# Two transformer blocks on one core: seven shared 4 KB weight slots, deferred decays and transposes, and softmaxes used one step later

## The chip, the cores and the metric

The kernel runs on one core of a Trainium2 chip. The metric is device time in microseconds (us). TensorE (PE) multiplies, VectorE (DVE), ScalarE (ACT) and GpSimd (POOL) do the element-wise work, and SyncE (SP) issues nearly all DMAs, in the order of its queue. On each engine the instructions run in one fixed order.

## The reference, cut to what matters

The input is one sequence of 256 tokens with 1024 features. A first block of two hybrid layers and a second block of two attention layers follow each other; all is float32. Only the first block's mixer and feed-forward part matter here:

```python
def hybrid_layer(x, c, ...):
    mod = jax.nn.silu(c) @ ada_w + ada_b
    sh_m, sc_m, gt_m, sh_f, sc_f, gt_f = jnp.split(mod[:, None, :], 6, axis=-1)
    h = rms_norm(x, norm_mix) * (1 + sc_m) + sh_m
    (aq, ak, av, bq, bkc, bvc, bks, bvs, bkw, bvw, bg, cqkv, cz, ca, cb) = jnp.split(h @ w_in, points, axis=-1)
    o_a = banded_attention(...)      # window 128, with a sink logit
    o_b = nsa_mixer(...)             # compressed, selected and window branch, gated
    o_c = gated_delta_net(cqkv, ca, cb, cz, ...)   # a unit lower triangular system per chunk of 64
    x = x + gt_m * (jnp.concatenate([o_a, o_b, o_c], axis=-1) @ w_out)
    h = rms_norm(x, norm_ffn) * (1 + sc_f) + sh_f
    gate, up = jnp.split(h @ w_gate_up, 2, axis=-1)
    return x + gt_f * ((jax.nn.silu(gate) * up) @ w_down)
```

`ada_w` is 1024 x 6144 for each layer; `compress_tokens` of the compressed branch multiplies 15 windows of 2048 values by `cmp_k_w1` and `cmp_v_w1`, 2048 x 256 each.

## The kernel before, in words

Every float32 product of the projections is made of three PE passes over a high and a low half of each operand (lines L209 to L211). `load` brings a weight tile from HBM; `cut` makes the high half `wh` on ACT (L193) and the low half `wl` on DVE, or on POOL for some tiles (L194). Weight tiles are named `ws`: 8 KB per partition, 1 MB in all, three buffers; one of them holds two blocks of the projection `proj_fm`, or four of the eight steps of `proj_tm`. The compress weights take the same three buffers (as `w`). `wh` and `wl` have five buffers each.

The modulation `mod` is a product of one row with a matrix and is made on DVE: `mod_unit` loads two tiles `aw` of 512 KB (three buffers of 4 KB per partition) and multiplies and sums each in one instruction of 128x1024 (L351). Of the units some are made before the first layer; the others stand in a list, and `pump(n)` takes the next n of them wherever it is called: in the first layer's mixer, and in the passes of the feed-forward parts.

`mixer1` is one layer's mixer. Its order in the program: the convolved blocks of the gated delta net that `begin` made, the token-major projection `w_misc`, `gdn_begin` (gates and decays), the heads `bq0` to `ak` (each a projection, a copy `raw` and a rotation with the product `pr`, L371), among them `gdn_cols` and `gdn_pairs`, then `gdn_solve`, `cmp_mlp`, the softmaxes, and the remaining projections. `gdn_pairs` makes for each of two chunks the products `kk` (L789), the matrix `mt` (L792), from it `xx` (L802, L804), and its transpose `xp` on PE (L809). `gdn_solve` inverts the triangular matrices by doubling in five levels (`yp`, `y`, `zp`, L831 to L850) and a last one (L856 to L861). `cmp_mlp` is the compress multiplication `hp` (L981).

An attention step is `scores` (`sc`, L384), `probs` (`lg` and the column sums `st`, on DVE and ACT, L395 to L412), `turned` (the transposes `tp`, L420, and their copy) and `pv` (`ot`, L430 and L432). The list `two` collects two heads, and `values` uses them up at once. The gated delta net's later blocks go through `conv`, whose second halves wait in the list `late` until the next block has been projected; `vp` (L738) is a transpose of theirs. `ffn` has 22 passes per layer; each loads a gate-and-up tile `w_gu`, and every second one two blocks of `w_dn`.

The program is written in this order, and a scheduler decides at build time, by its own costs and by the buffers that are free, how the instructions stand on each engine. Two lines set the rings:

```python
    def load(self, src, shape, pool=None, tag="ws", bufs=3):
            a = self.load(self.io["ada_w"][l, u, :, i], (P, 1024), tag="aw") if aw is None else aw[:, i, :]
```

## Time and profile before

| | us |
|---|---|
| median of 3 runs | 1479.03 (1478.26 to 1482.65) |
| the profiled execution, its time | 1478.33 |
| its span, first to last instruction | 1476.6 |
| PE busy | 1411.6 (96%) |
| DVE busy | 1141.2 (77%) |
| ACT busy | 822.0 (56%) |
| POOL busy | 123.2 (8%) |

The mean granted clock of TensorE is 0.988 of full speed. The chain that ended last lies on PE for 72% of the span, on DVE for 16%, on ACT for 5%; DMA holds 2%. Times in the rows below count from the span's first instruction: the first layer's mixer takes the first 217 us or so, its feed-forward part follows up to 408, the second layer's mixer up to some 606, and its feed-forward part and the second block the rest. In a row of the timeline, "[3.84 <-DVE xx L804]" says that the engine was idle for 3.84 us before it and what ended that; the number behind a tile's name is left out. A float32 product that isn't made of halves counts as two rows of the trace.

### The profile page before, as it was taken

To read this page: it belongs to the slowest core of one execution; us is meant where nothing else is said; L and a number is where in the kernel's file an instruction comes from. 1 tells how busy PE (TensorE), PEld (TensorE's weight loads), DVE (VectorE), ACT (ScalarE), POOL (GpSimd) and SP (SyncE) were. 2 spreads that over 40 slices of the span, in tenths; PEclk is the share of its full clock that TensorE was granted. 3 is DMA by queue.
4 is the path that set the end of the run, shared out by engine and by line. 5 is a ranking of instruction groups with operands and counts; after the bars stand their busy time and mean duration, and the time that the engine had idled before them with its cause. 6 is when DMAs were issued, how large, how long until landed. Compare 5 with 4: busy or idle time off the path is not lost.

```text
span 1476.6 us, 29198 instructions
## 1 busy us (share of the span) xinstructions
PE 1411.6 (96%) x11742; PEld 1313.8 (89%) x11742; DVE 1141.2 (77%) x2357; ACT 822.0 (56%) x1585; POOL 123.2 (8%) x125
## 2 busy tenths in 40 slices
PE   5989999999999899999999999999999999999998
PEld 3877789999988678999999888899999888899997
DVE  7888899998987467865566896697788665888875
ACT  3637765444473577644446555565555655755554
POOL 0141010000124200100001001100000100100000
PEclk9999999999999999999999999999999999999999
DMA  9576567899733522659744434279673342655520
GB/s 376 209 272 231 190 233 274 328 372 334 254 106 118 177 86 87 230 186 170 271 163 139 155 143 172 87 268 211 240 256 141 115 143 87 242 215 191 195 101 30
DMA packets 58266, 287.79 MB, mean 195 GB/s; under 512 B 6701, under 2 KB 12721, under 8 KB 35346
## 3 DMA queue, kind: packets, MB, share of 16 engines
q1 hardware_dynamic: 56722, 279.63, 52.5%
q0 software_dynamic: 1408, 6.29, 3.5%
q8 instruction: 92, 1.51, 0.4%
q14 instruction: 44, 0.36, 0.1%
HBM read 277.97 MB, written 7.34 MB: 193 GB/s over the span
## 4 chain that ended last, share of the span: by engine, by line
PE 72%; DVE 16%; ACT 5%; issue 3%; DMA 2%; POOL 1%; SPq 0%; POOLq 0%; DVEq 0%; ACTq 0%
PE pf L209 13%; PE pf L210 13%; PE pf L211 13%; PE acc L210 5%; PE acc L209 5%; PE acc L211 5%; DVE wl L194 3%; PE sc L384 2%; PE ot L430 2%; DVE aw L351 1%; DVE hl L205 1%; PE zp L831 1%; PE tp L420 1%; ACT wh L193 1%; POOL sq L67 1%
## 5 line engine op out<-in xcount | busy, mean ns | idle before, releaser
L209 PE MATMUL pf<-hh,wh 128*128 128x256 f32 (+1 forms) x1976 | 564.6, 286 | 2.7 <-ACT rb L138 1.2
L210 PE MATMUL pf<-hl,wh 128*128 128x256 f32 (+1 forms) x1976 | 561.1, 284 | 5.4 <-DVE hl L205 5.3
L211 PE MATMUL pf<-hh,wl 128*128 128x256 f32 (+1 forms) x1976 | 559.8, 284 | 0.0
L193 ACT CAST wh<-ws 128x1024 fp32r<-128x1024 f32 (+1 forms) x299 | 308.7, 1037 | 234.8 <-PE pf L210 166.5
L194 DVE TENSOR_TENSOR wl<-ws,wh 128x1024 fp32r<-128x1024 f32 (+1 forms) x289 | 350.7, 1215 | 82.8 <-ACT wh L193 80.8
L209 PEld LDWEIGHTS pf<-hh,wh 128*128 128x128 f32 x1976 | 374.8, 190 | 12.0 <-issue 6.8
L210 PEld LDWEIGHTS pf<-hl,wh 128*128 128x128 f32 x1976 | 375.3, 190 | 10.3 <-DVE hl L205 8.3
L211 PEld LDWEIGHTS pf<-hh,wl 128*128 128x128 f32 x1976 | 374.8, 190 | 2.2 <-issue 1.6
L209 PE MATMUL acc<-ah,dh 128*128 128x256 f32 x704 | 197.8, 283 | 2.3 <-ACT ah L201 2.1
L210 PE MATMUL acc<-al,dh 128*128 128x256 f32 x704 | 198.3, 282 | 1.7 <-DVE al L202 1.7
L211 PE MATMUL acc<-ah,dl 128*128 128x256 f32 x704 | 198.2, 282 | 0.0
L194 DVE TENSOR_TENSOR dl<-wd,dh 128x1024 fp32r<-128x1024 f32 x88 | 107.9, 1226 | 42.8 <-ACT dh L193 42.8
L210 PEld LDWEIGHTS acc<-al,dh 128*128 128x128 f32 x704 | 133.8, 190 | 2.4 <-DVE al L202 2.3
L209 PEld LDWEIGHTS acc<-ah,dh 128*128 128x128 f32 x704 | 132.9, 190 | 3.1 <-ACT ah L201 3.1
L211 PEld LDWEIGHTS acc<-ah,dl 128*128 128x128 f32 x704 | 133.7, 190 | 0.0
L193 ACT CAST dh<-wd 128x1024 fp32r<-128x1024 f32 x88 | 92.1, 1047 | 71.3 <-PE acc L210 70.7
L67 POOL TENSOR_TENSOR sq<-sq 128x256 f32<-128x256 f32 x52 | 43.0, 827 | 778.4 <-ACT sq L65 772.6
L351 DVE SCALAR_TENSOR_TENSOR aw<-aw,sc 128x1024 f32<-128x1024 f32 x80 | 101.0, 1267 | 3.6 <-DMA aw<-in_ada_w 3.6
L1121 DVE SCALAR_TENSOR_TENSOR fy<-fu,cw,fy 128x254 f32<-128x254 f32 (+1 forms) x176 | 83.5, 480 | 5.4 <-ACT fy L1119 2.7
L400 ACT ACTIVATE lg<-lg,st 128x128 f32<-128x128 f32 x112 | 50.1, 449 | 21.2 <-DVE st L395 16.3
L1102 DVE TENSOR_TENSOR a<-pf,rb 128x258 f32<-128x258 f32 x88 | 37.1, 424 | 30.8 <-PE pf L211 28.4
L1119 ACT ACTIVATE fy<-fu,cw 128x256 f32<-128x256 f32 x88 | 52.4, 600 | 9.4 <-DVE fu L1118 9.1
(371 smaller groups left out, 2163.4 us busy)
## 6 DMA issues: line engine op xcount, KB each, us to landing
ws<-in_w_gu SPq DMA_DIRECT2D x44, 1024.0 KB, 6.1
wd<-in_w_dn SPq DMA_DIRECT2D x44, 1024.0 KB, 4.9
ws<-in_w_up SPq DMA_DIRECT2D x44, 1024.0 KB, 4.8
aw<-in_ada_w SPq DMA_DIRECT2D x80, 512.0 KB, 6.2
ws<-in_w_fm SPq DMA_DIRECT2D x16, 1024.0 KB, 7.8
ws<-in_w_even SPq DMA_DIRECT2D x12, 1024.0 KB, 4.8
ws<-in_ada_w SPq DMA_DIRECT2D x8, 1024.0 KB, 8.6
w<-in_cmp_w SPq DMA_DIRECT2D x8, 1024.0 KB, 5.0
```

The source lines that it names most:

```text
L67: (nc.vector if i else nc.gpsimd).tensor_tensor(sq, sq, last, op=ALU.add)
L193: nc.scalar.copy(wh, ws)
L194: (eng or nc.vector).tensor_tensor(wl, ws, wh.bitcast(F32), op=ALU.subtract)
L209: mm(out, lhsT=lh, rhs=rh, start=start, stop=False, **kw)
L210: mm(out, lhsT=lh, rhs=rl, start=False, stop=False, **kw)
L211: mm(out, lhsT=ll, rhs=rh, start=False, stop=stop, **kw)
L351: nc.vector.scalar_tensor_tensor(a, a, 1.0, self.sc, op0=ALU.mult, op1=ALU.mult, accum_out=acc)
L384: self.nc.tensor.matmul(sc[half][:, out], lhsT=q[r, t], rhs=k[r, 0:n], start=True, stop=True)
L400: nc.scalar.activation(lg[:, rng[i]], lg[:, rng[i]], AF.Exp, bias=nm[:, i:i + 1], scale=-1.0, accum_out=den[:, i:i + 1])
L1102: nc.vector.tensor_tensor(t[j], ps[j], self.rb, op=ALU.mult)
L1119: nc.scalar.activation(y, u, AF.Identity, scale=w[:, 2:3], bias=w[:, 3:4])
L1121: nc.vector.scalar_tensor_tensor(y[:, d:S], u[:, 0:S - d], w[:, 2 - d:3 - d], y[:, d:S], op0=ALU.mult, op1=ALU.add)
```

## The change

All weight tiles become 4 KB per partition, 512 KB in all, in one ring of seven that weights, `ada_w` tiles and compress weights share; the buffers of `wh` and `wl` go from five to six. What was one request of 1 MB is two of 512 KB. `proj_tm` is cut into steps, so that others can take them one by one. `gdn_begin` returns its decays as a function, which is called with the next block's late work. The transposes `xp` go from `gdn_pairs` to the start of `gdn_solve`. The compress weights are loaded and used in quarters. The attention is a loop of six steps: step i+1's scores and softmaxes are requested after step i's values, two projection blocks or `w_z` steps stand between a softmax and its transposes, the late halves of the convolved blocks follow one step later, two units of the modulation are pumped per step in the first layer, and the compressed branch's softmax is split into `cmp_probs` and `turn`. The second block's code is changed only through `load`, `cut`, and `proj_tm`.

```diff
-    def load(self, src, shape, pool=None, tag="ws", bufs=3):
+    def load(self, src, shape, pool=None, tag="ws", bufs=7):
...
-    def cut(self, ws, pool=None, tag="w", bufs=5, eng=None):
+    def cut(self, ws, pool=None, tag="w", bufs=6, eng=None):
...
+        for _ in self.proj_tm_steps(outs, src, n, pre):
+            pass
+    def proj_tm_steps(self, outs, src, n, pre=None):
...
-            if k % 4 == 0:
-                ws = pre[k // 4] if pre else self.load(src[k // 4], (P, 4, n))
-            wh, wl = self.cut(ws[:, k % 4:k % 4 + 2, :])
+            wh, wl = self.cut(pre[k // 2] if pre else self.load_tm(src, k, n))
...
+            yield
+    def load_tm(self, src, k, n):
+        return self.load(src[k // 4, :, k % 4:k % 4 + 2], (P, 2, n))
...
-        return self.load(src[i0:i0 + n].rearrange("b p k m -> p b k m"), (P, n, KT, P))
+        return [self.load(src[i0 + j], (P, KT, P)) for j in range(n)]
...
-            a = self.load(self.io["ada_w"][l, u, :, i], (P, 1024), tag="aw") if aw is None else aw[:, i, :]
+            a = self.load(self.io["ada_w"][l, u, :, i], (P, 1024)) if aw is None else aw[:, i, :]
...
-            def conv(i0, blocks):
-                for j, ps in enumerate(blocks):
-                    if i0 > 2:
-                        flush()
-                    late.append(self.gdn_conv(l, sp, pp, g, i0 + j, ps))
-                    if j % 2:
-                        self.pump(1 if l == 0 and i0 > 2 else 0)
...
-            conv(0, ahead)
+            for j, ps in enumerate(ahead):
+                late.append(self.gdn_conv(l, sp, pp, g, j, ps))
...
-                pre = [self.load(io["w_misc"][0, i], (P, 4, 276)) for i in range(2)]
-                for i in (12, 14):
-                    ws[i] = self.load_blocks(w_fm, i)
+                pre = [self.load_tm(io["w_misc"][0], k, 276) for k in range(0, KT, 2)]
+                ws[12] = self.load_blocks(w_fm, 12)
...
+                ws[14] = self.load_blocks(w_fm, 14)
...
-            self.gdn_begin(l, sp, pp, ab, g)
+            late.append(self.gdn_begin(l, sp, pp, ab, g))
...
-            two = []
...
-                values()
-                self.split(ot, oh[blk], ol[blk])
...
+            band, caus = ((self.c(o, 128), self.c(o + 128, 256)) for o in (C_BAND, C_CAUS))
+            v2 = g["v2"]
+            def attend(i):
+                if i < 2:
+                    sc = self.scores(pp, rot[f"aq{i}"], self.kk[2])
+                    hs = (i, i + 2)
+                    return [self.probs(sp, sc[n], *band, nsink=self.nsink[:, l, h:h + 1], sink=self.sink[:, l, h:h + 1])
+                            for n, h in enumerate(hs)]
+                blk, br = divmod(i - 2, 2)
+                sc = self.scores(pp, rot[f"bq{blk}"], self.kk[br])
+                return [self.probs(sp, sc[n], *caus, gate=g["gates"][:, :, 4 * (br + 1) + 2 * blk + n])
+                        for n in range(2)]
+            def value(i, pts, ot, pc):
+                blk, br = divmod(i - 2, 2)
+                if i >= 2 and br == 0:
+                    nc.tensor.matmul(ot, lhsT=v2[:, 2 * blk:2 * blk + 2, :].rearrange("p h d -> p (h d)"), rhs=pc,
+                                     start=True, stop=False, skip_group_check=True)
+                two = []
+                for n, pt in enumerate(pts):
+                    r = slice(64 * n, 64 * n + 64)
+                    vs = r if i < 2 else slice(128 + 64 * br, 192 + 64 * br)
+                    two.append((ot[r, :], pt, vt[0][:, vs], vt[1][:, vs], i < 2, i < 2 or br == 1))
+                self.pv(two)
+                if i < 2 or br == 1:
+                    n = i if i < 2 else 2 + blk
+                    self.split(ot, oh[n], ol[n])
+            pz = []
+            def fills():
+                for i in range(4, 12, 2):
+                    for j, ps in enumerate(self.blocks(w_fm, i, pool=(1,), ws=ws.get(i))):
+                        late.append(self.gdn_conv(l, sp, pp, g, i + j, ps))
+                        yield
+                pz.extend(self.pj.tile([P, 512], F32, tag="pj", name="pz") for _ in range(2))
+                yield from self.proj_tm_steps(pz, io["w_z"][l], 512)
+            fill, pc = fills(), None
+            lgs = attend(0)
+            for i in range(6):
+                for _ in range(2):
+                    next(fill)
+                if i == 0:
+                    cmp = self.cmp_probs(sp, pp, g, raw)
+                pts = [self.turned(sp, pp, lg) for lg in lgs]
+                if i == 1:
+                    pc = cmp()
+                for one in late[0:2 * min(i, 1)]:
+                    late.pop(0)()
+                if i in (0, 1, 2, 4):
+                    ot = pp.tile([P, S], F32, tag="o", name="ot", bufs=1)
+                value(i, pts, ot, pc)
+                if i < 5:
+                    lgs = attend(i + 1)
+                    self.pump(2 if l == 0 else 0)
...
...
+        def decays():
+            self.gdn_decays(sp, pp, g)
+        return decays
+    def gdn_decays(self, sp, pp, g):
+        nc, gg = self.nc, g["gg"]
...
-            xp = pp.tile([P, 256], F32, tag="g", name="xp", bufs=3)
-            for h in range(4):
-                for r in half:
-                    nc.tensor.matmul(xp[r, 64 * h:64 * h + 64], lhsT=a[r, h, :], rhs=self.ident[r, r], start=True,
-                                     stop=True)
-            nc.scalar.copy(flat(b), xp)
...
+        for c in range(2):
+            xp = pp.tile([P, 256], F32, tag="g", name="xp", bufs=3)
+            for h in range(4):
+                for r in half:
+                    nc.tensor.matmul(xp[r, hs(h)], lhsT=xt[c][r, h, :], rhs=self.ident[r, r], start=True, stop=True)
+            nc.scalar.copy(flat(x[c]), xp)
...
-            for u in range(2):
-                w1 = self.wp.tile([P, 8, 256], F32, tag="ws", name="w1", bufs=3)
-                nc.sync.dma_start(w1, io["cmp_w1"][l, j, u])
-                for c in range(8):
-                    q = 32 * (c % 4)
-                    nc.tensor.matmul(hp[q:q + 15, :], lhsT=win[:, 8 * u + c, :], rhs=w1[:, c, :],
-                                     start=u == 0 and c < 4, stop=u == 1 and c >= 4, skip_group_check=True)
+            for u in range(4):
+                w1 = self.load(io["cmp_w1"][l, j, u // 2, :, u % 2 * 4:u % 2 * 4 + 4], (P, 4, 256))
+                for c in range(4):
+                    q = 32 * c
+                    nc.tensor.matmul(hp[q:q + 15, :], lhsT=win[:, 4 * u + c, :], rhs=w1[:, c, :], start=u == 0,
+                                     stop=u == 3, skip_group_check=True)
...
-        tp = pp.tile([64, 256], F32, tag="s", name="ctp")
...
-            nc.tensor.transpose(tp[:, tb * P:tb * P + P], e[:, tb].rearrange("p h n -> p (h n)"), self.ident)
-        pc = sp.tile([64, 256], F32, tag="ctk", name="pc")
-        nc.scalar.copy(pc, tp)
-        return pc
+        def turn():
+            tp = pp.tile([64, 256], F32, tag="g", name="ctp", bufs=3)
+            for tb in range(2):
+                nc.tensor.transpose(tp[:, tb * P:tb * P + P], e[:, tb].rearrange("p h n -> p (h n)"), self.ident)
+            pc = sp.tile([64, 256], F32, tag="ctk", name="pc")
+            nc.scalar.copy(pc, tp)
+            return pc
+        return turn
...
-                    ws = self.load(w_in[f], (P, 2, KT, P))
+                    ws = [self.load(w_in[f][:, j], (P, KT, P)) for j in range(2)]
...
-                    ps = [self.proj_fm(self.cut(ws[:, j]), *((pp, "pb") if f % 2 else (self.pj, "pj")), n=n)
+                    ps = [self.proj_fm(self.cut(ws[j]), *((pp, "pb") if f % 2 else (self.pj, "pj")), n=n)
```

The order on the engines moves at three places that the prediction speaks of. On SP, in the first layer, from the compress weights on, before (`cmp_w` are the compress weights, `kk`, `ctk` and `ctv` copies between partitions):

```order
L978 DMA w_1205<-in_cmp_w 128x2048
L185 DMA aw<-in_ada_w 128x1024
L978 DMA w_1215<-in_cmp_w 128x2048
L978 DMA w_1234<-in_cmp_w 128x2048
L586 DMA kk_88<-kk_88 64x256
L587 DMA kk_89<-kk_89 64x256
L960 DMA ctk<-ctk 64x256
L961 DMA ctv<-ctv 64x256
L185 DMA aw<-in_ada_w 128x1024 x6
L978 DMA w_1244<-in_cmp_w 128x2048
L185 DMA ws<-in_w_fm 128x2x1024
L185 DMA aw<-in_ada_w 128x1024
```

and after the change:

```order
L185 DMA ws<-in_cmp_w 128x1024 x4
L981 DMA ctk<-ctk 64x256
L982 DMA ctv<-ctv 64x256
L585 DMA kk_88<-kk_88 64x256
L586 DMA kk_89<-kk_89 64x256
L185 DMA ws<-in_cmp_w 128x1024 x4
L185 DMA ws<-in_w_fm 128x1024 x2
L185 DMA ws<-in_ada_w 128x1024 x8
L185 DMA ws<-in_w_fm 128x1024 x2
L185 DMA ws<-in_ada_w 128x1024 x4
L185 DMA ws<-in_w_fm 128x1024 x2
L185 DMA ws<-in_ada_w 128x1024 x4
```

Seven requests of `ada_w` stood among the compress weights; now none does.

On DVE, in the first layer, from the matrix `mt` of the first chunk on, before:

```order
L792 SCALAR_TENSOR_TENSOR mt_751<-kk,gc_580,dec_485 128x128 x4
L351 SCALAR_TENSOR_TENSOR aw,mod<-aw,sc 128x1024
L802 TENSOR_TENSOR xx_757<-md_756,lv 128x256
L354 TENSOR_TENSOR mod<-mod,adab 128x2
L351 SCALAR_TENSOR_TENSOR aw,mod<-aw,sc 128x1024
L804 TENSOR_TENSOR xx_757<-ident,xx_757 64x256 x2
L373 TENSOR_TENSOR rp_835<-pr,cs 128x256
L351 SCALAR_TENSOR_TENSOR aw,mod<-aw,sc 128x1024
L792 SCALAR_TENSOR_TENSOR mt_778<-kk,gc_580,dec_492 128x128 x4
```

and after (L813, L823 and L825 are L792, L802 and L804 of before):

```order
L813 SCALAR_TENSOR_TENSOR mt_761<-kk,gc_588,dec_522 128x128 x4
L813 SCALAR_TENSOR_TENSOR mt_778<-kk,gc_588,dec_529 128x128 x3
L823 TENSOR_TENSOR xx_767<-md_766,lv 128x256
L813 SCALAR_TENSOR_TENSOR mt_778<-kk,gc_588,dec_529 128x128
L825 TENSOR_TENSOR xx_767<-ident,xx_767 64x256 x2
L823 TENSOR_TENSOR xx_784<-md_783,lv 128x256
L379 TENSOR_TENSOR rp_825<-pr,cs 128x256
L825 TENSOR_TENSOR xx_784<-ident,xx_784 64x256 x2
```

The three products of `ada_w` (L351) are gone from between, and both chunks' `mt` and `xx` stand together.

On PE, at the same place, behind the 24 projection instructions of one block, before:

```order
L371 MATMUL pr<-raw,cs 128x256
L809 MATMUL xp<-ident,xx_757 64x64
L789 MATMUL kk<-kT_307 128x128
L809 MATMUL xp<-ident,xx_757 64x64 x7
L789 MATMUL kk<-kT_318 128x128
L789 MATMUL kk<-kT_328 128x128
L789 MATMUL kk<-kT_339 128x128
L371 MATMUL pr<-raw,cs 128x256
L981 MATMUL hp<-w_1205,win 15x256 x8
L981 MATMUL hp<-w_1215,win 15x256 x8
L809 MATMUL xp<-ident,xx_784 64x64
```

and after:

```order
L377 MATMUL pr<-raw,cs 128x256
L852 MATMUL xp<-ident,xx_767 64x64 x7
L377 MATMUL pr<-raw,cs 128x256
L852 MATMUL xp<-ident,xx_767 64x64
L852 MATMUL xp<-ident,xx_784 64x64
L1001 MATMUL hp<-ws,win 15x256
L852 MATMUL xp<-ident,xx_784 64x64 x7
L846 MATMUL yp<-xx_767,ms 64x64 x8
L1001 MATMUL hp<-ws,win 15x256 x4
L846 MATMUL zp<-y,xx_767 64x64 x8
```

The second chunk's `kk` now stand ahead of the 24 projections, and the compress multiplication is spread over the inverse.

## Rows read from the trace of the kernel before

**Rows 1.** The page, busy time and share of the span by engine

```profile
PE 1411.6 (96%) x11742; PEld 1313.8 (89%) x11742; DVE 1141.2 (77%) x2357; ACT 822.0 (56%) x1585; POOL 123.2 (8%) x125
```

**Rows 2.** Busy time by stretch: us, PE, PEld, DVE, ACT, POOL, granted clock, DMA share, GB/s

```profile
75.00:92.00 17.00, 12.62 (x109) 9.55 (x108) 12.36 (x30) 3.60 (x10) 3.98 (x4) 0.80 0.68 209
92.00:124.00 32.00, 29.75 (x611) 24.69 (x610) 28.48 (x66) 17.44 (x46) 18.06 (x11) 1.00 0.89 318
124.00:184.00 60.00, 59.44 (x376) 45.17 (x375) 51.09 (x157) 47.01 (x138) 2.42 (x2) 1.00 0.56 188
225.00:408.00 183.00, 182.06 (x1516) 181.63 (x1516) 171.94 (x307) 86.31 (x125) 5.34 (x2) 1.00 0.86 314
500.00:536.00 36.00, 31.98 (x198) 25.53 (x198) 21.42 (x61) 22.61 (x62) 4.96 (x2) 0.86 0.23 86
```

**Rows 3.** The same view, the two stretches at half clock

```profile
82.80:89.60 6.80, 5.60 (x38) 3.98 (x42) 4.82 (x13) 0.98 (x3) 0.00 (x0) 0.50 0.69 227
509.50:519.70 10.20, 10.20 (x33) 6.42 (x34) 4.65 (x20) 5.42 (x17) 0.00 (x0) 0.50 0.09 39
```

**Rows 4.** Timeline, PE, first layer: start, us, line, tiles, [idle before]

```profile
77.79 0.28 PE L209 MATMUL pf<-hh,wh 128*128 128x256 f32 x1
...
79.45 0.28 PE L211 MATMUL pf<-hh,wl 128*128 128x256 f32 x1
79.56 0.59 PE L371 MATMUL pr<-raw,cs 128*128 128x256 f32 x2
84.00 0.44 PE L809 MATMUL xp<-ident,xx 64*64 64x64 f32 x2 [3.84 <-DVE xx L804]
...
91.52 0.32 PE L809 MATMUL xp<-ident,xx 64*64 64x64 f32 x2 [0.53 <-DVE xx L804]
...
120.73 0.50 PE L856 MATMUL yp<-xx,mt 64*64 64x64 f32 x5 [1.89 <-issue]
```

**Rows 5.** Timeline, DVE, first layer, from `mt` to `xx`

```profile
77.52 1.11 DVE L792 SCALAR_TENSOR_TENSOR mt<-kk,gc,dec 128x128 f32<-128x128 f32 x4
80.05 1.31 DVE L351 SCALAR_TENSOR_TENSOR aw<-aw,sc 128x1024 f32<-128x1024 f32 x1 [1.42 <-DMA aw<-in_ada_w]
...
81.29 0.93 DVE L802 TENSOR_TENSOR xx<-md,lv 128x256 f32<-128x256 f32 x1
...
82.28 1.23 DVE L351 SCALAR_TENSOR_TENSOR aw<-aw,sc 128x1024 f32<-128x1024 f32 x1
...
83.44 0.87 DVE L804 TENSOR_TENSOR xx<-ident,xx 64x256 f32<-64x256 f32 x2
```

**Rows 6.** Timeline, PE, second layer, four waits

```profile
463.70 0.30 PE L809 MATMUL xp<-ident,xx 64*64 64x64 f32 x2 [1.09 <-DVE xx L804]
...
488.73 0.68 PE L831 MATMUL zp<-y,xx 64*64 64x64 f32 x16 [1.49 <-ACT y L840]
...
507.75 0.84 PE L420 MATMUL tp<-ident,lg 128*128 128x128 f32 x3 [2.06 <-ACT lg L412]
...
532.99 0.33 PE L738 MATMUL vp<-ident,cv 128*128 128x128 f32 x1 [1.74 <-DVE cv L732]
```

**Rows 7.** Timeline, POOL and DVE, second layer, two places

```profile
503.89 2.47 POOL L194 TENSOR_TENSOR wl<-ws,wh 128x1024 fp32r<-128x1024 f32 x1 [5.24 <-ACT wh L193]
...
504.04 2.35 DVE L398 TENSOR_SCALAR st<-st,nsink 128x2 f32<-128x2 f32 x1
...
528.46 2.49 DVE L729 SCALAR_TENSOR_TENSOR cv<-cu,cw,cv 128x253 f32<-128x253 f32 x1
```

**Rows 8.** Groups by line, 225:408; DMA issues, 225:408, then 75:125: KB, us to landing

```profile
L351 DVE SCALAR_TENSOR_TENSOR aw<-aw,sc 128x1024 f32<-128x1024 f32 x52 | 63.0, 1218 | 2.2 <-DMA aw<-in_ada_w 2.2
...
aw<-in_ada_w SPq DMA_DIRECT2D x49, 512.0 KB, 7.7
ws<-in_w_gu SPq DMA_DIRECT2D x18, 1024.0 KB, 8.4
...
aw<-in_ada_w SPq DMA_DIRECT2D x14, 512.0 KB, 5.9
```

More of the change, by code (lines that the diff above doesn't have):

```diff
@@ L250, in blocks @@
         for j in range(n):
-            yield self.proj_fm(self.cut(ws[:, j], eng=self.nc.gpsimd if j in pool else None))
+            yield self.proj_fm(self.cut(ws[j], eng=self.nc.gpsimd if j in pool else None))
     def first(self, src, eng=None):
-        ws = self.load(src, (P, 2, KT, P))
-        return [self.cut(ws[:, j], eng=eng) for j in range(2)]
+        ws = [self.load(src[:, j], (P, KT, P)) for j in range(2)]
+        return [self.cut(w, eng=eng) for w in ws]
     def warm(self, func, after):
@@ L438, in out_proj @@
         for g in range(2):
-            ws = self.load(src[g], (P, 4, 4, P))
+            ws = [self.load(src[g][:, i:i + 2], (P, 2, 4, P)) for i in (0, 2)]
             if turn is not None and g == 1:
@@ L444, in out_proj @@
                 if i % 2 == 0:
-                    wh, wl = self.cut(ws[:, i:i + 2], **kw)
+                    wh, wl = self.cut(ws[i // 2], **kw)
                 pool, tag, bufs = rings[m % len(rings)]
@@ L634, in mixer1 @@
-            conv(4, (ps for i in (4, 6) for ps in self.blocks(w_fm, i, pool=(1,), ws=ws.get(i))))
-            pc = self.cmp_probs(sp, pp, g, raw)
-            c0, c1 = self.c(C_CAUS, 128), self.c(C_CAUS + 128, 256)
-            for blk in range(2):
-                ot = pp.tile([P, S], F32, tag="o", name="ot", bufs=1)
-                nc.tensor.matmul(ot, lhsT=g["v2"][:, 2 * blk:2 * blk + 2, :].rearrange("p h d -> p (h d)"), rhs=pc,
-                                 start=True, stop=False, skip_group_check=True)
-                for br in range(2):
-                    sc = self.scores(pp, rot[f"bq{blk}"], self.kk[br])
-                    for half in range(2):
-                        h = 2 * blk + half
-                        r = slice(64 * half, 64 * half + 64)
-                        lg = self.probs(sp, sc[half], c0, c1, gate=g["gates"][:, :, 4 * (br + 1) + h])
-                        vs = slice(128 + 64 * br, 192 + 64 * br)
-                        two.append((ot[r, :], lg, vt[0][:, vs], vt[1][:, vs], False, br == 1))
-                    values()
-                    self.pump(1 if l == 0 else 0)
-                self.split(ot, oh[2 + blk], ol[2 + blk])
@@ L653, in mixer1 @@
-            conv(8, (ps for i in (8, 10) for ps in self.blocks(w_fm, i, pool=(1,))))
-            pz = [self.pj.tile([P, 512], F32, tag="pj", name="pz") for _ in range(2)]
-            self.proj_tm(pz, io["w_z"][l], 512)
+            band, caus = ((self.c(o, 128), self.c(o + 128, 256)) for o in (C_BAND, C_CAUS))
[10 more added lines that the diff above has]
+                        for n in range(2)]
@@ L661, in mixer1 @@
                 nc.vector.scalar_tensor_tensor(sz, th, 1.0, pz[tb], op0=ALU.add, op1=ALU.mult)
-                self.pump(1 if l == 0 else 0)
             flush()
@@ L1014, in cmp_probs @@
         nc = self.nc
-        cp = pp.tile([P, 2, 4, 16], F32, tag="s", name="cp")
+        cp = pp.tile([P, 2, 4, 16], F32, tag="g", name="cp", bufs=3)
         for tb in range(2):
```

14 lines of the change are left out of this document (removed).

## The prediction

> **What bounds the kernel now.** First the busy shares: TensorE (PE) is busy for 1411.6 of 1476.6 us [rows 1], so waits of PE hold 65 us in the whole program, and no change of buffers or order can give back more than these, plus what is lost where the clock is granted at half. Then the busy time by stretch, to see where the two lie [rows 2]. The first layer's start of the inverse (75 to 92 us) has PE at 12.62 of 17 us; its attention (124 to 184) and its feed-forward part (225 to 408) have PE at 59.44 of 60 and 182.06 of 183. In that last one VectorE (DVE) is busy for 171.94 of 183 us and the DMA engines for 0.86 of it: there is nothing to win there and something to lose. The second layer's first softmaxes (500 to 536) have PE at 31.98 of 36 at a mean clock of 0.86. In two stretches the granted clock is 0.50, the lower of its two levels (1.2 for 2.4 GHz): 82.8 to 89.6 and 509.5 to 519.7 us [rows 3]. Each begins behind a wait of PE: the first begins inside the 3.84 us for `xx`, the second after the 2.06 us for `lg` [rows 4, 6].
>
> The third view is the timeline, for who is late at these two places. At 84.00 PE waits 3.84 us for `xx` [rows 4]. On DVE the chain `mt`, `xx`, `xx` that makes it holds two ada_w products in its middle: one waits 1.42 us for its DMA and takes 1.31, the other takes 1.23, together 4.0 us beside 2.9 us of the chain's own work [rows 5]. At 507.75 PE waits 2.06 us for `lg` [rows 6]; the chain behind it had a DVE instruction of two columns that took 2.35 us, beginning 0.15 us after a cut on GpSimd (POOL) of 2.47 us [rows 7]. At 528.46 another DVE instruction takes 2.49 us, and PE's 1.74 us for `cv` follows it [rows 6, 7].
>
> **The change part by part.** The sum is made against the profiled execution, 1478.3 us, 0.7 us below the median of 1479.03.
>
> *Transposes and requests.* In the changed order `mt` to the second `xx` has no ada_w product between, since the ada_w requests stand behind all compress weights on SP; and PE has the other chunk's `kk`, 24 projections and `pr` ahead of the first `xp`. After the last `kk` DVE needs 1.11 (`mt`), 0.93 and 0.87 us, plus some of the second chunk's `mt`, say 3.1 to 3.7 us. PE's cover is 24 projections, 0.119 us apart (15 of them lie between 77.79 and 79.45, so 1.66/14), and one `pr` of 0.59 [rows 4], 3.4 us. So the wait of 3.84 goes: **-3.8**. With it goes the dip: PE worked 5.60 us in it [rows 3], half of which at full clock is **-2.8**. Of the 0.53 us behind it [rows 4] I take half, **-0.3**; of the 1.89 us before the last `yp` [rows 4] I take **-1.0**, because PE and DVE have `zt` and `mt` in another order there, but nothing says that their latency is covered. At the second layer the same move takes the `xp` wait of 1.09 [rows 6]: **-1.1**. The 1.49 us for `y` there stays: weights still come late to ACT. **0**.
>
> *What the requests do in the inverse.* By the order the compress multiplication `hp` uses up whole 1 MB tiles now, 16 instructions in a row; afterwards each 512 KB quarter is used inside the inverse, one between steps. It frees the slot that the next ada_w or w_fm tile waits for. DVE, busy for 28.48 of 32 us there [rows 2], then stands before a product until the tile is there: 5.9 us from issue to landing for 512 KB in this stretch [rows 8]. If the slots come early enough it costs nothing; at worst every wait of DVE reaches PE, in my count of the order 5 us. The nearest row is the 0.53 us that `xx` is late at 91.52 [rows 4], four or so times: **+2** (0 to +5).
>
> *First layer's attention.* By the order some five products less are done when the inverse ends. They come after it, at 1.21 to 1.23 us each 6.1 us, to a DVE busy for 51.09 of 60 [rows 2, 5]: 57.2, just under full. POOL cuts also move from the inverse to here, and two such cuts each held one DVE instruction 2.3 us in the second layer [rows 7]. Later use of the softmaxes covers part of it. **+2** (0 to +5).
>
> *Later use of the softmaxes, second layer.* PE now has 30 projections and the `cp` group between the last `sc` and the first `tp` where it had 28; that alone is 0.3 us, but the next pairs have 37 to 44. The first `tp` also depends on POOL's cut, which has moved behind the first probabilities. I take **-1.8** of the 2.06 and **-1.5** of the 1.74 us before `vp`, which now comes an iteration later (bounds 0 and the whole of each). The dip behind them: PE worked 10.20 us at half [rows 3], **-5.1**. But the same work is denser or thinner elsewhere, and one new stretch at half is likely, priced as the one of rows 2, (1 - 0.80) x 17 = 3.4 us: **+3.4** (0 to +5.1).
>
> *Seven slots of 4 KB.* Feed-forward, first layer: 52 products in 21 passes of 183/21 = 8.7 us, 2.5 of them a pass [rows 8], plus two halves of the gate weights: 4.5 tiles a pass. A slot comes round in 7/4.5 x 8.7 = 13.6 us. Before, an ada_w slot came round in 3/2.5 x 8.7 = 10.4 us and DVE waited for it 2.2 us in all, with landings of 7.7 us, and 8.4 for the 1 MB tiles [rows 8]. So the ada_w tiles get 3 us more of lead; the weights, which had three slots for themselves (26 us), get much less, and still 13.6 against 8.4. I take **0** (0 to +10). Second block and the other passes: the order there is the same, 1 MB becomes two halves, and PE waits little. **0** (-1 to +3). The sixth buffer of `wh` and `wl` lets ACT and DVE cut one tile further ahead; no row shows PE waiting for that: **0**.
>
> A rule speaks against the change: the Trainium skill, "DMA: Bandwidth & Descriptors", section "Measured (HBM→SBUF, 128 partitions, SWDGE, issued from GpSimd)", asks to batch DMAs to at least 1 MiB for 75% of peak; these go to half. The rows do not bear it out so far: in one stretch 512 KB lands in 7.7 us beside 8.4 for 1 MB with several on the way [rows 8]. By the rows the term is 0, by the rule it is the second rival's.
>
> Sum: -3.8 - 2.8 - 0.3 - 1.0 - 1.1 + 2 + 2 - 1.8 - 1.5 - 5.1 + 3.4 = **-10.0, 1468.3 us**, which I give 0.45 (with 4 us to either side).
>
> **The rivals.**
> *The ring starves DVE (slower).* In the first feed-forward part DVE has 183 - 171.94 = 11.1 us free, 0.53 a pass [rows 2]. One shared ring means that a gate-weight tile which is held until its cut is done also delays the next ada_w tile. Up to 0.53 us of waiting a pass costs nothing; beyond it each microsecond costs 21. The gain is used up at 0.53 + 10.0/21 = 1.0 us a pass; at 1.5 it is 21 x 0.97 = 20.4, **1489 us**. For it: the DMA engines are at 0.86 and DVE already waited 2.2 us there. Against: 13.6 us for landings of 8. 0.11.
>
> *Smaller transfers make the DMA engines the bound (slower).* At 0.86 [rows 2] they have room for 1/0.86 = 1.16 times their time. If halves cost 30% more time on the engines, the stretch takes 183 x 0.86 x 1.3 = 205 us, 22 more: **1490 us**. Against: the landings named above. 0.04. This is how the rule of the Trainium skill named above ("DMA: Bandwidth & Descriptors", the section on what was measured) would show in this kernel.
>
> *Waits come back elsewhere (no change).* The inverse and the attention each cost their +5, the `tp` wait stays with its dip, no new one: -3.8 - 2.8 - 0.3 - 1.0 - 1.1 + 10 - 1.5 = -0.5, **1477.8 us**, and a stall in a few passes of the ring brings it to 1482. For: DVE at 57 of 60. 0.18.
>
> *All goes (faster).* No new wait, no new dip: -10.0 - 2 - 2 - 3.4 = -17.4, **1460.9 us**. For: PE's waits are then covered by the fill at every softmax. 0.20.
>
> *The change does not do what it says.* The order shows the moves, so only a latency could undo them: 1478. 0.02.
>
> **How the numbers follow.** About 0.3%, 4.4 us, is what a measurement of this kernel can tell from no change: 1474.6 to 1483.5 around the median. Faster: 0.43 of the forecast, 0.20 of all-goes, 0.04 of no change, 0.67. Slower: both slower rivals and the tail of the third, 0.16. Same: 0.17. The range leaves out the two slower rivals and some of the tails: from 1456, 5 us under all-goes, to 1482.
>
> **What would show it.** Right: no wait of PE before `xp` at 84 us and a clock of 1.00 there; no wait before the first `tp` at some 500 us and at most one short stretch at half between 440 and 540; in the first inverse waits of DVE or ACT on ada_w or w_fm tiles of 1 to 3 us each, with PE losing some 2. DVE over 55 of the 60 us of the first attention. Wrong: a wait on DMA of more than 0.53 us a pass before the ada_w products of the first feed-forward part; landings of 512 KB over 10 us there; a DMA share of 1.0; new stretches at half in the inverse.

## The result, and the profile after

The changed kernel takes 1464.84 us (median of 6 runs, 1458.0 to 1468.85) beside 1478.64 for the kernel before: a ratio of 0.9898, 95% interval 0.9872 to 0.9925. A second set gave 1465.35 and 0.9916 (0.9891 to 0.9940). The forecast was 1468.3, in a range of 1456 to 1482. The profiled execution took 1463.45 us.

First the page of the changed kernel: span, busy time, and the DMA queue that carries the weights (packets, MB, time of its packets as a share of 16 engines' span).

```profile
span 1461.7 us, 29723 instructions
...
PE 1407.1 (96%) x11742; PEld 1313.3 (90%) x11742; DVE 1140.4 (78%) x2357; ACT 823.7 (56%) x1585; POOL 120.0 (8%) x125
...
q1 hardware_dynamic: 75730, 279.64, 55.2%
```

The same queue of the kernel before:

```profile
q1 hardware_dynamic: 56722, 279.63, 52.5%
```

PE does the same instructions; its idle time fell from 65.0 [rows 1] to 54.6 us. The stretches of [rows 2], at the same times (the work in them has moved by up to 6 us):

```profile
75.00:92.00 17.00, 16.99 (x281) 13.63 (x280) 10.56 (x28) 4.23 (x11) 5.80 (x8) 1.00 0.52 167
92.00:124.00 32.00, 28.75 (x471) 23.30 (x468) 25.52 (x61) 14.72 (x40) 9.85 (x7) 0.95 0.71 245
124.00:184.00 60.00, 55.22 (x323) 43.02 (x324) 51.36 (x157) 44.00 (x130) 4.81 (x2) 0.89 0.68 221
225.00:408.00 183.00, 179.64 (x1480) 178.82 (x1480) 165.81 (x288) 87.42 (x122) 5.96 (x4) 0.99 0.86 307
500.00:536.00 36.00, 34.88 (x284) 28.54 (x281) 25.19 (x87) 27.92 (x84) 2.69 (x1) 1.00 0.24 83
```

The start of the inverse is full and at full clock (1.00), and so, nearly, are the second layer's softmaxes; but the first layer's attention, full before, now has PE idle for 4.8 us at a mean clock of 0.89. To see where time went, the span is cut at events of PE that every kernel here has: the last `gtp` of the first layer's scan, the last `acc` of its feed-forward part, the last `zt` of the second inverse, the last `gtp` of the second scan, the first `acc` behind it, the end. Stretches in us, from one profiled execution each (e1 to e12 are the experiments; where a profile lies more than 2 us from its kernel's median, the last column says so):

| | scan 1 | ffn 1 | inverse 2 | scan 2 | to ffn 2 | rest | span |
|---|---|---|---|---|---|---|---|
| before | 208.7 | 205.8 | 86.3 | 89.0 | 32.1 | 854.7 | 1476.6 |
| changed | 212.3 | 207.1 | 84.5 | 83.3 | 25.9 | 848.6 | 1461.7 |
| e5 changed again | 209.7 | 208.5 | 84.7 | 83.2 | 25.9 | 850.0 | 1461.9 |
| e1 ring only | 214.0 | 203.9 | 86.9 | 88.0 | 25.8 | 848.7 | 1467.4 (5 us under) |
| e2 order only | 203.0 | 210.8 | 86.3 | 86.6 | 31.9 | 855.7 | 1474.4 |
| e3 old attention | 212.8 | 207.5 | 84.9 | 87.0 | 25.1 | 850.6 | 1467.9 |
| e4 no POOL cuts | 209.0 | 204.0 | 83.5 | 83.7 | 25.5 | 849.7 | 1455.4 |
| e6 five cut buffers | 209.8 | 206.0 | 86.3 | 86.6 | 25.9 | 849.9 | 1464.5 |
| e7 ring of nine | 203.8 | 206.1 | 89.8 | 87.5 | 27.2 | 849.8 | 1464.2 (3 us over) |
| e8 transposes back | 209.4 | 208.6 | 88.5 | 83.4 | 25.9 | 851.0 | 1466.7 |
| e9 before, no POOL cuts | 213.3 | 207.2 | 86.3 | 86.2 | 30.3 | 856.6 | 1479.8 |
| e10 nine, no POOL cuts | 206.7 | 203.9 | 88.8 | 81.4 | 25.8 | 849.4 | 1456.0 |
| e11 rings of six and three | 206.2 | 213.4 | 89.6 | 83.4 | 30.8 | 862.7 | 1486.1 (2 us over) |
| e12 rings of seven and two | 207.2 | 217.7 | 86.9 | 85.0 | 30.7 | 849.0 | 1476.5 |

Before to changed: +3.6, +1.3, -1.8, -5.7, -6.2, -6.1, together -14.9. Twelve of these lie in the last two stretches, where I had forecast nothing, and the first layer's mixer, for which I had forecast -3.9, got slower. Two executions of the changed kernel (second and third row) differ by up to 2.6 us in a stretch, so smaller differences say little.

The marks are events of PE, and work can move across them. The last three stretches of the kernel before, then of the changed kernel, by engine:

```profile
500.80:589.80 89.00, 84.91 (x556) 69.01 (x555) 58.40 (x173) 63.10 (x178) 4.96 (x2) 0.94 0.26 93
589.80:621.90 32.10, 30.02 (x218) 28.84 (x217) 28.32 (x41) 20.56 (x35) 6.23 (x7) 0.89 0.62 231
621.90:1476.60 854.70, 833.24 (x6708) 797.24 (x6706) 626.24 (x1191) 471.80 (x808) 38.12 (x49) 1.00 0.51 170
```

```profile
503.90:587.20 83.30, 81.81 (x584) 68.90 (x581) 64.34 (x186) 62.57 (x177) 2.69 (x1) 1.00 0.39 127
587.20:613.00 25.80, 23.79 (x188) 22.49 (x187) 25.51 (x41) 19.53 (x34) 7.17 (x7) 1.00 0.74 269
613.00:1461.70 848.70, 832.63 (x6708) 797.75 (x6706) 627.04 (x1193) 472.09 (x807) 38.16 (x49) 1.00 0.54 172
```

So the three do not gain in the same way. In the last one PE does the same instructions and is idle for 16.1 us in place of 21.5: waits make 5.4 of the 6.1. In the stretch before it PE is idle for 2.1 and 2.0 us, the same; what is gone is 6.8 us at a granted clock of 0.50 (608.5 to 615.3 in the kernel before), worth 3.4 us, and some 30 PE instructions, which now run ahead of the mark, in the second scan. There the gain of 5.7 is made in spite of them: the 10.2 us at half and 2.6 us of PE's idle time are gone.

The first layer's mixer, cut at the last `zt` of its inverse, takes 124.1 and then 84.6 us before, 118.0 and then 94.3 after (116.0 and 93.6 in e5). From that `zt` to the end of the scan, before and after:

```profile
124.10:208.70 84.60, 82.80 (x563) 67.03 (x561) 73.10 (x215) 59.70 (x172) 2.38 (x1) 1.00 0.57 190
```

```profile
118.00:212.30 94.30, 89.33 (x584) 74.21 (x581) 83.07 (x236) 67.11 (x190) 7.19 (x3) 0.93 0.62 201
```

PE's idle time grows from 1.8 to 5.0 us, 13.7 us are at half clock (worth 6.8), where none were, and PE and DVE each do 21 instructions more. The timeline of PE there shows what came and what went:

```profile
81.70 0.73 PE L852 MATMUL xp<-ident,xx 64*64 64x64 f32 x14
...
94.18 0.39 PE L209 MATMUL pf<-hh,wh 128*128 128x256 f32 x1 [2.09 <-ACT wh L193]
...
136.28 0.47 PE L759 MATMUL vp<-ident,cv 128*128 128x128 f32 x1 [2.71 <-ACT vs L760]
...
158.51 0.61 PE L771 MATMUL ssp<-one,csq 128*128 128x1 f32 x4 [1.73 <-ACT csq L766]
```

The 3.84 us before `xp` [rows 4] are gone. New are 2.09, 2.71 and 1.73 us; behind the first the clock is granted at 0.50 from 95.3 for 3.4 us, behind the second from 136.3 for 10.2. Behind the second is a chain over three engines: POOL, DVE, ACT.

```profile
130.03 2.41 POOL L194 TENSOR_TENSOR wl<-ws,wh 128x1024 fp32r<-128x1024 f32 x1 [9.14 <-ACT wh L193]
...
129.98 2.55 DVE L1057 TENSOR_TENSOR ce<-ce,cst 128x64 f32<-128x64 f32 x2
...
133.47 0.40 ACT L406 ACTIVATE lg<-lg,st 128x128 f32<-128x128 f32 x1 [1.87 <-DVE st L404]
```

A POOL cut of 2.41 us, and DVE's two instructions of 64 columns beside it last 2.55 us together. The softmax's sums come late, ACT waits for them 1.87 us, and the copy `vs` that frees PE's `vp` stands behind it. That is the pattern of [rows 7], one layer earlier. The POOL cut is not all that can make this wait, though: in e10, which has no such cut there, PE waits 2.55 us for the same `vs`.

In the second layer the three waits of [rows 6] that I had counted on stand without one:

```profile
469.08 0.67 PE L852 MATMUL xp<-ident,xx 64*64 64x64 f32 x14
...
508.48 0.53 PE L426 MATMUL tp<-ident,lg 128*128 128x128 f32 x3
...
517.15 0.38 PE L759 MATMUL vp<-ident,cv 128*128 128x128 f32 x2
```

In the stretches that the forecast left at 0, the kernel before had these waits (its timeline, PE; all three lie in the table's last stretch), none of which is over 0.5 us in the changed kernel:

```profile
710.64 0.38 PE L209 MATMUL acc<-ah,dh 128*128 128x256 f32 x1 [1.42 <-ACT ah L201]
...
964.93 0.39 PE L210 MATMUL pf<-hl,wh 128*128 128x256 f32 x1 [1.00 <-DVE hl L205]
...
968.19 0.61 PE L81 MATMUL nps<-one,sq 128*128 128x1 f32 x4 [0.81 <-POOL sq L67]
```

And the first feed-forward part of the changed kernel, for [rows 8] (groups by line, then DMA issues, 225 to 408 us):

```profile
L357 DVE SCALAR_TENSOR_TENSOR ws<-ws,sc 128x1024 f32<-128x1024 f32 x46 | 55.6, 1218 | 0.0
...
ws<-in_ada_w SPq DMA_DIRECT2D x41, 512.0 KB, 6.3
ws<-in_w_gu SPq DMA_DIRECT2D x40, 512.0 KB, 6.0
```

The ada_w products wait for no DMA (2.2 us before), and the half tiles land in 6.0 us where the whole ones took 8.4. There are also fewer products in the way, 46 for 52: eight of all 96 now run in the second layer (558.8 to 606.1 us). So it is in every trace with a shared ring; with two rings none runs so late.

### The profile page after: what moved, and what is told of

Same layout as the page of the kernel before. It is cut to its first block, busy times and chain, and to the rows that moved or that the text cites. A ratio compares the mean times of both kernels' runs of the same rounds, so it can differ in the third digit from the quotient of the medians.

```text
span 1461.7 us, 29723 instructions
## 1 busy us (share of the span) xinstructions
PE 1407.1 (96%) x11742; PEld 1313.3 (90%) x11742; DVE 1140.4 (78%) x2357; ACT 823.7 (56%) x1585; POOL 120.0 (8%) x125
## 3 DMA queue, kind: packets, MB, share of 16 engines
q1 hardware_dynamic: 75730, 279.64, 55.2%
## 4 chain that ended last, share of the span: by engine, by line
PE 76%; DVE 12%; ACT 5%; DMA 4%; issue 2%; POOL 1%; POOLq 0%; DVEq 0%; ACTq 0%; SPq 0%
PE pf L209 14%; PE pf L210 14%; PE pf L211 14%; PE acc L209 5%; PE acc L211 5%; PE acc L210 5%; DMA ws<-in_w_up 3%; DVE wl L194 2%; DVE ws L357 2%; ACT wh L193 1%; PE sc L390 1%; PE ops L209 1%; DVE hl L205 1%; PE ops L210 1%; PE ops L211 1%
## 5 line engine op out<-in xcount | busy, mean ns | idle before, releaser
L357 DVE SCALAR_TENSOR_TENSOR ws<-ws,sc 128x1024 f32<-128x1024 f32 x96 | 118.8, 1251 | 6.4 <-ACT sc L482 5.3
```

The lines of the kernel that those rows point to most:

```text
L357: nc.vector.scalar_tensor_tensor(a, a, 1.0, self.sc, op0=ALU.mult, op1=ALU.mult, accum_out=acc)
```

## The experiments

**Ring alone and order alone.** e1 takes the change of buffers, tile sizes and compress quarters only; e2 the deferred decays, transposes and the attention loop only. Of e1, against the kernel before:

```diff
-    def load(self, src, shape, pool=None, tag="ws", bufs=3):
+    def load(self, src, shape, pool=None, tag="ws", bufs=7):
...
-            a = self.load(self.io["ada_w"][l, u, :, i], (P, 1024), tag="aw") if aw is None else aw[:, i, :]
+            a = self.load(self.io["ada_w"][l, u, :, i], (P, 1024)) if aw is None else aw[:, i, :]
...
```

e2 has these lines, `cut`, `proj_tm`'s tiles and the whole compress weights as the kernel before, and all else as the changed one.

> Only the ring: 4 KB tiles in seven shared slots, six buffers of wh and wl, compress weights in quarters; decays, transposes and attention as before. Theory A (the gain is in the order: xp transposes and softmax use): about the time before, between -2 and +3 us, with the xp wait of some 4 us at 80 to 85 us and the tp wait of 2 us near 505 us still there, each with a stretch at half clock. Rival B (the ring gives the gain, since feed-forward and second block, whose order is as before, ended 6 us nearer): -6 us or more, over half of the 13.8.

Measured: 1474.55 us, ratio 0.9968 (0.9951 to 0.9985): 4.6 us by the medians, a third of the gain. Its profile has 0.60 us before `xp` in the first layer where the kernel before has 3.84, and none before `tp`; in the second layer `xp` still waits 1.30 us. So Theory A is wrong about these waits, and the gain is short of Rival B's. The ring alone takes them: no ada_w product stands between `mt` and `xx` in its trace, and POOL's cut that stood beside that softmax, at 503.89 [rows 7], now comes behind it:

```profile
514.48 2.40 POOL L194 TENSOR_TENSOR wl<-ws,wh 128x1024 fp32r<-128x1024 f32 x1 [14.39 <-ACT wh L193]
```

The ring alone also has the 6 us in each of the last two stretches; and it costs 5 us up to the first scan. Its profiled execution is 5 us under its median, so part of what the table gives it may be that execution's alone.

> Only the order: deferred decays, transposes at the start of the inverse, softmaxes used a step later, modulation pumped by step; weight tiles of 8 KB in three slots, ada_w in its own three, compress weights whole, as before. Theory A: -8 to -14 us, the xp and tp waits gone. Rival B: -4 to -7 us, with feed-forward and second block as long as before. Theory C (the two need each other: with three 8 KB slots the requests come too late for the new order): 0 or slower, with waits on DMA in the first layer.

Measured: 1475.91 us, ratio 0.9992 (0.9969 to 1.0014): not to be told from the kernel before. By the table it gains 5.7 us up to the first scan, about what I had summed for the first layer (3.9), and gives 5.0 back in the feed-forward part. The last two stretches are as before, as Rival B has it. In the second layer the `tp` wait and the cause of it are still there, though softmaxes are used a step later (DVE, then PE, of e2):

```profile
503.43 2.34 DVE L403 TENSOR_SCALAR st<-st,nsink 128x2 f32<-128x2 f32 x1
...
507.14 0.84 PE L425 MATMUL tp<-ident,lg 128*128 128x128 f32 x3 [1.25 <-ACT lg L417]
```

So the two parts are worth more together (13 to 14 us) than the sum of what each brings alone, 6 to 8 us (4.6 and, by its ratio or its median, 1.2 to 3.3); the intervals only just leave room for that.

**The old attention on the changed kernel.**

```diff
-            lgs = attend(0)
-            for i in range(6):
...
+            for blk in range(2):
...
+                sc = self.scores(pp, rot[f"aq{blk}"], self.kk[2])
...
+                values()
```

> The changed kernel with the attention of before (softmaxes used at once, pump as before), ring, decays and transposes as changed. Theory A: the second layer's 2 us tp wait and its 10 us at half come back (+9 us), the first layer's new vp wait of 2.71 us with 10 us at half goes (-8 us): about +1 us on the changed kernel, within 3. Rival B: within 1 us of the changed kernel. If the first layer's loss comes from the modulation's later requests instead, +9 us.

Measured: 1469.02 us, ratio 0.9941 (0.9922 to 0.9960), about 4 us over the changed kernel. The place is the second scan (87.0 for 83.3, of which the stretch behind it gives 0.8 back); the first layer does not get faster without the new attention, which speaks against the loop as the cause of its loss. The `tp` wait did not come back.

**POOL's cuts.** e4 changes the changed kernel, as shown; e9 takes the same `pool=(1,)` out of the two `conv` calls of the kernel before:

```diff
-                    for j, ps in enumerate(self.blocks(w_fm, i, pool=(1,), ws=ws.get(i))):
+                    for j, ps in enumerate(self.blocks(w_fm, i, ws=ws.get(i))):
```

> The changed kernel, with the second block of each pair in the attention cut on DVE (1.22 us) and not on POOL (2.41 us), eight cuts in the two layers. Theory A (a POOL cut holds a DVE instruction for its whole time, and that made the 2.71 us wait for vp at 136 us and the half clock behind it): -5 to -8 us on the changed kernel, no DVE instruction of small size over 1.5 us in the attention. Rival D (DVE is simply full there, 51 of 60 us): 0 to +3 us, the wait stays or moves.

Measured: 1458.78 us (4 runs, 1457.3 to 1459.99), ratio 0.9870 (0.9843 to 0.9897): by the medians 6 us faster than the changed kernel, by the ratios 4 to 7, with intervals that touch the first one's. The 2.71 us wait is gone. But the gain doesn't lie where I looked for it: 0.7 to 3.3 us up to the first scan, 3.1 to 4.5 in the feed-forward stretch, whose start had a wait of 1.75 us for POOL's sum of squares and 3.4 to 6.8 us at half clock in the changed kernel, and neither here.

> The kernel before, with its eight attention cuts of the two layers on DVE (1.22 us) and not on POOL (2.4 to 2.5 us): no ring, no new order. Theory G (the second layer's tp wait of 2.06 us, its 10 us at half and the vp wait of 1.74 us come from POOL cuts that hold DVE, and not from softmaxes used too soon): -5 to -9 us on the kernel before, those waits under 0.5 us. Theory A (softmax used too soon): -1 to -2 us, the tp wait stays over 1 us with its stretch at half.

Measured: 1480.62 us, ratio 1.0019 (1.0006 to 1.0033). Theory G is right at its place and wrong in the sum. Of e9 the first and the second scan's stretch, and of the kernel before the second:

```profile
123.50:213.30 89.80, 84.90 (x562) 69.89 (x559) 74.84 (x218) 59.61 (x172) 0.00 (x0) 0.94 0.55 186
506.70:592.90 86.20, 84.19 (x574) 68.63 (x573) 60.65 (x179) 63.85 (x179) 0.00 (x0) 1.00 0.30 103
```

```profile
500.80:589.80 89.00, 84.91 (x556) 69.01 (x555) 58.40 (x173) 63.10 (x178) 4.96 (x2) 0.94 0.26 93
```

In the second layer the clock goes from 0.94 to 1.00 and the `tp` and `vp` waits go (2.8 us). In the first, where DVE has the ada_w products as well, a new wait of 1.20 us for `lg` and 10.2 us at half cost more. In the changed kernel the same move did not cost in the first layer (e4). So where a cut is better on POOL hangs on what stands beside it there; that DVE being full decides it is argued, not shown.

**The changed kernel again, and the sizes of its rings.**

> The changed kernel itself, beside the next three on one chip: a ratio of 0.990 to the kernel before, within 0.003, if its first result holds; its profile shows again the wait for vp near 136 us if that wait is its own, and not of one execution.

Measured: 1465.35 us, 0.9916 (0.9891 to 0.9940); the vp wait is there with 2.69 us.

```diff
-    def cut(self, ws, pool=None, tag="w", bufs=6, eng=None):
+    def cut(self, ws, pool=None, tag="w", bufs=5, eng=None):
```

> The changed kernel with five buffers of wh and wl, as before, ring of seven kept. Theory E (the sixth buffer lets the next stage's weights be cut before the residual ends, so that no cut stands between the hl of a norm: it removed the waits of 1.42 and 0.91 near 710, 1.00 and 0.81 near 965 and 0.96 and 0.81 near 1277 us, 5.9 us): +4 to +7 us on the changed kernel, with those waits back. Rival B (the ring brings the weights earlier, and that removed them): 0 to +1 us.

Measured: 1466.12 us, 0.9921 (0.9897 to 0.9945). Theory E falls: the waits near 710, 965 and 1277 us stay away with five buffers. The second scan takes 86.6 for 83.3 without the sixth, other stretches less, and in all it is worth nothing that these runs can tell.

```diff
-    def load(self, src, shape, pool=None, tag="ws", bufs=7):
+    def load(self, src, shape, pool=None, tag="ws", bufs=9):
```

> The changed kernel with five buffers of wh and wl, and the 8 KB that this frees given to the ring: nine slots. Theory E: as with five buffers and seven slots, +4 to +7 us on the changed kernel, because slots are not what is short; only the wait of ACT for w_fm in the first inverse (3.21 us, PE 2.09) goes, -2. Rival B (lead of requests is what counts): faster than the changed kernel, by 2 us or more.

Measured (five cut buffers as well): 1462.56 us, 0.9901 (0.9878 to 0.9924), not clearly apart from the changed kernel. Up to the first scan it is 6 to 8 us faster; in the second inverse a wait of 2.48 us and 6.8 us at half clock take 5 back, and the second scan 4 more, as e6 with its five cut buffers loses 3 there.

> The changed kernel with nine slots, five buffers of wh and wl, and no POOL cuts in the attention. If the cure of the POOL cuts (6 us) and that of the ring of nine in the first layer (6 us nearer at the end of its scan) add up: 1452 to 1457 us, ratio 0.983. If they cure the same waits: 1458 to 1460, as with seven slots and no POOL cuts.

Measured: 1458.55 us, 0.9882 (0.9863 to 0.9901). The two don't add up; it equals e4 within what can be told. By the medians both beat the changed kernel by 6 to 7 us, with the same memory; e10's interval overlaps that kernel's, so this much is likely and not shown.

**The transposes back in the pairs** (ring and attention as changed):

```diff
+            xp = pp.tile([P, 256], F32, tag="g", name="xp", bufs=3)
+            for h in range(4):
...
             md.append(d)
```

> The changed kernel with the transposes xp back in the pairs, before the second chunk's products kk. Theory A as the prediction had it (the move of the transposes takes the 3.84 us wait and the 2.8 us at half): +5 to +7 us on the changed kernel. Theory F (the later ada_w requests took the two products out of the chain, which is enough, as the run of the ring alone has no wait there either): 0 to +2 us; in the second layer the 1.1 to 1.3 us wait before xp comes back.

Measured: 1466.77 us, 0.9922 (0.9891 to 0.9952), 1.4 us over the changed kernel. Theory F holds: without the move `xp` waits 0.61 us in the first layer, and not 3.84. In the second it comes back, larger than it was:

```profile
465.98 0.33 PE L830 MATMUL xp<-ident,xx 64*64 64x64 f32 x2 [2.36 <-DVE xx L825]
```

with 3.4 us at half; the second inverse takes 88.5 for 84.5.

**One ring or two.** e11 gives the ada_w tiles their own three slots again and leaves six to the weights; e12 gives two and seven. Both have five buffers of `wh` and `wl`, so all of e7, e11 and e12 use the same memory as the kernel before.

```diff
-    def load(self, src, shape, pool=None, tag="ws", bufs=7):
+    def load(self, src, shape, pool=None, tag="ws", bufs=6):
...
-            a = self.load(self.io["ada_w"][l, u, :, i], (P, 1024)) if aw is None else aw[:, i, :]
+            a = self.load(self.io["ada_w"][l, u, :, i], (P, 1024), tag="aw", bufs=3) if aw is None else aw[:, i, :]
```

> The changed kernel with 4 KB tiles in two rings, six slots for weights and three for ada_w as before, five buffers of wh and wl (the same memory as nine shared slots, and the same as before). Theory H (small tiles give the gain behind the first layer, and sharing the ring costs it 5 to 8 us in the first layer's attention, where ada_w tiles take the weights' slots): the first layer's scan ends at 204 to 206 us after the start and not at 210 to 212, and the total is 1459 to 1463. Rival (sharing, and the lead that it gives, is what brings the gain): waits near 710, 965 and 1277 us are back, 1468 us or more.

Measured: 1486.01 us, ratio 1.0059 (1.0039 to 1.0079): 23 us over e7, which differs by the sharing alone, and slower than the kernel before. The first scan ends at 206.2 as Theory H says, but the feed-forward stretch (213.4), the second inverse (89.6) and the rest (862.7) are worse than in every other kernel of the table, or nearly. It is also 10 us over e2, which has the same order, the same bytes in each ring, and whole tiles: halving the requests alone does not pay.

> The changed kernel with 4 KB tiles in two rings again, seven slots for weights and two for ada_w, five buffers of wh and wl: the same memory as six and three. Theory I (six 4 KB slots are one too few for the weights, and the seventh is what the sharing gave them wherever no ada_w tile is on the way): the second block, from the first downward product of the second layer to the end, takes some 849 us as with seven or nine shared slots and not 858 as with six; in all 1462 to 1470 us, if two ada_w slots do not hold up the first feed-forward part, there at worst +5. Rival (sharing itself, that requests stand in one order on one ring): the second block stays at 856 us or more, the total at 1480 or more.

Measured: 1478.63 us, ratio 1.0007 (0.9984 to 1.0030). The rest takes 849.0 us, as with seven and nine shared slots, and not 862.7: Theory I holds there, the seventh slot is what the second block gains. But two slots starve the ada_w products of the first feed-forward part, far worse than I allowed (groups by line, 230 to 410 us, and its stretch):

```profile
L357 DVE SCALAR_TENSOR_TENSOR aw<-aw,sc 128x1024 f32<-128x1024 f32 x48 | 60.1, 1252 | 19.0 <-DMA aw<-in_ada_w 18.9
```

```profile
233.20:424.90 191.70, 182.93 (x1489) 180.96 (x1488) 171.18 (x303) 82.20 (x123) 6.52 (x4) 0.98 0.87 305
```

18.9 us of waiting for DMA over 21 passes is 0.9 a pass, and between these two marks it takes 191.7 us for 179.2. The stretch to the second feed-forward part takes 30.7 and 30.8 us in e12 and e11, near the 32.1 of before: its 6 us come with the shared ring only. They are the two things found above: each of the five traces with two rings has 3.4 to 6.8 us at half clock there, of the nine with a shared ring only e7 has (3.4); and PE starts 197 to 215 instructions in that stretch with two rings, 183 to 189 with one. What in the ring brings that about is open. So neither of these two splits serves both: the weights want seven slots wherever no ada_w tile is on the way, and the ada_w tiles want more than two where they are. The shared ring gives each what it needs at its time.

## Why the prediction was right, and where it was not

The range held the time and the sign was right. That the size was near (10.0 forecast against 13.8 and 12.8) is in good part luck: the first layer's mixer came out 7.5 and 4.9 us worse than its terms, and 11 to 12 us came from stretches that had been put at 0.

- *Transposes and requests, "the wait of 3.84 goes", with its stretch at half*: it went, and nothing came in its place at `xp`. The cause was named half right. The later requests alone do it but for 0.6 us (e8, e1), and so does the changed order with the ada_w tiles' own ring kept (e2, 0.52 us left at a later `xp`); the move is worth 4 us in the second layer only. The +2 for late weights in the inverse came as forecast: ACT waits 3.21 us for a `w_fm` tile and PE 2.09 behind it (1.17 in e5). A new stretch at half in the inverse, named as a sign of being wrong, is there for 3.4 us in one of the two executions. Up to the last `zt` of the first inverse the mixer gained 6.1 and 8.1 us, for a forecast of 5.9.
- *First layer's attention, +2 (0 to +5)*: the step that failed. With the inverse's term the forecast up to the first scan was -3.9; measured +3.6 and +1.0. From the `zt` on it is +9.7 and +9.0 us for the +2. I had DVE at 57 of 60 and said "just under full"; it was only 51.36, and still PE waits 2.71 us there, behind a POOL cut, with 6.8 to 10.2 us at half clock. I had priced waits there, and no stretch at half. e2 shows that the order alone does reach -5.7 there; what is lost comes with the ring of seven, and with nine slots it does not come (203.8). The POOL cuts do not make it: without them (e4) it is 93.7 us from the `zt` on, beside 93.6 and 94.3. With rings of their own for the ada_w tiles it is 84.4 to 86.5 (e12, e2, e11). What in the shared ring does it is not settled: with nine slots it is 86.9 (e7) and 91.5 (e10), and with the transposes back 87.4 (e8).
- *Softmaxes, second layer, -1.8, -1.5, -5.1 and +3.4, together -5.0*: measured -5.7, with 28 PE instructions more in the stretch. The dip of 10.2 us went as priced and the new one (+3.4) did not come. But the later use does not take the `tp` wait (e2 keeps 1.25 us of it); the POOL cut does, by its place in the order (e9), which the ring moved (e1, e3). The loop is worth 3.7 us there beside the ring (e3), though with five cut buffers the loop has 86.6 as well (e6).
- *Seven slots, second block and the rest, 0 (-1 to +3)*: the second step that failed. It measured -6.2 in the stretch to the second feed-forward part and -6.1 behind it. I had looked for waits in the first feed-forward part and found none to win; I had not listed the waits of 0.8 to 1.4 us at the later stages' starts (PE's idle time in the last stretch fell by 5.4), and had not seen that the three ada_w slots lie idle in all of the second block, so that sharing them is a seventh slot for the weights (e12). And the forecast counts two stretches at half clock, where the trace of the kernel before has six: 24.8 and 31.6 us (3.4 each), 82.8, 509.5, 608.5 (6.8) and the last 6.5 us. The one at 608.5 was worth 3.4 us and went.
- *First feed-forward part, 0 (0 to +10)*: right (+1.3 and +2.7, at its start). No product waits for DMA, though six of the products were no longer there to wait. The slower rival was a real mechanism: it is what e12 does, at 0.9 us a pass. The rival's formula, 21 x (0.9 - 0.53), gives 8 of the 12.5 us that the stretch grew by; the 6.8 us that its clock spent at half account for 3.4 more.
- *Smaller transfers*: the DMA engines' time went from 52.5% of 1476.6 to 55.2% of 1461.7 us, 4% more for the same bytes, and not 30% (e11: 54.0% of 1486.1 us, 3.5% more). The landings that the forecast held against the rule, 7.7 us beside 8.4 for twice the bytes, did not speak to it. The rule of the Trainium skill, "DMA: Bandwidth & Descriptors", section "Measured (HBM→SBUF, 128 partitions, SWDGE, issued from GpSimd)", is to batch DMAs to 1 MiB or more. These traces agree with its direction and give the price here, where SP issues: 3 to 4%, in a kernel whose busiest stretch has the engines at 0.86 before and after.

## What to carry to other kernels

A buffer that serves one phase only is idle memory in all others; one ring of equal tiles lends it out, and that was worth 16 to 23 us beside the same bytes in two rings (e7 against e12 and e11). Look for what a ring of its own leaves unused, and list the small waits at every stage's start, and every stretch at half clock, before calling a stage full. And where an element-wise instruction can go to either of two engines that slow each other down, choose by what stands beside it at that moment, not once for the whole program: the same eight cuts moved to DVE gained some 6 us in one kernel (e4) and cost 2 in the other (e9).

## What the runs showed of the hardware

A subtraction of 128x1024 on POOL can hold up a DVE instruction until it ends: one of two columns took 2.34 and 2.35 us beside cuts of 2.48 and 2.47, and 0.22 elsewhere in the kernel before. It does not hold every one: beside a cut of 2.47 us at 496.18 in the kernel before, three that read the matmul result `zp` took 0.41 to 0.42 each. Half-size requests came in sooner under load (6.0 for 8.4 us) although together they cost the DMA engines 3 to 4% more. And a wait of 2.7 us of PE was followed by 6.8 us at the granted clock of 0.5 in one execution of the changed kernel, and by 10.2 in another; that alone is 1.7 us between two runs of the same kernel. Shorter waits can be followed by it too: in the kernel before one of 0.86 us at 608.17 was, by 6.8 us.
